# A third tile for every third gemv weight, laid in the attention's own pool

## The chip, the cores and the metric

The kernel runs on one core of a Trainium2 chip. What counts is the device time of one execution in microseconds; the figure before is the median of three runs.

## The reference, cut to what matters

A decoder trunk of two layers on 512 tokens of 1024 channels: layer 0 mixes tokens by stick-breaking attention, layer 1 by a diagonal state-space model, and each has a gated MLP with a short convolution behind it. Every sublayer is modulated by vectors computed from a conditioning vector `c`; that is the part that the change touches.

```
c_act = jax.nn.silu(c)
for i in range(DEPTH):
    mod = c_act @ w_mod[i] + b_mod[i]                      # (1024) @ (1024 x 6144)
    sh1, sc1, g1, sh2, sc2, g2 = jnp.split(mod, 6, axis=-1)
    h = modulate(rms_norm(x, norm_mix[i]), sh1, sc1)
    y = stick_breaking_attention(h, ...) if i == 0 else s5_ssm(h, ...)
    x = x + g1[:, None, :] * y
    h = modulate(rms_norm(x, norm_ffn[i]), sh2, sc2)
    x = x + g2[:, None, :] * conv_ffn(h, ...)
fin = c_act @ w_fin + b_fin
```

All arithmetic is float32; a product is made of three matmuls of split operands (high x high, low x high, high x low).

## The kernel before, in words

**The gemv.** `mod` and `fin` have 8192 outputs, which the kernel computes on DVE (VectorE), not on PE (TensorE): the transposed weights are cut into tiles of 128 outputs by 1024 inputs (512 KB), and for each tile one DVE instruction (L197, 1.2 us) multiplies it by `cact`, which holds silu(c) in every partition, and sums along the row into one column of `raw`. `gemv_step(col)` loads the tile and records that instruction; the tile is called `wg` and the column number (wg16 is the first one that the change concerns). The two tiles named `wg` that `gvp` (pool "gemv", right side of SBUF) holds are used in turn, so a load waits until the gemv two before it has been computed. When eight columns are done, `gemv_fin` (L204) adds the bias. The 16 columns that the first norm needs have a buffer of their own (`wgs`) and are not concerned.

**Where the gemvs stand in attention.** `bg(n)` takes the next n columns of a list and puts their gemvs at this place of the program. In attention the loads of wg16 to wg40 are issued by POOL (GpSimd, `queue=G`); all other large loads stand in the queue of SP (SyncE), each behind the one before it. POOL has nothing else to do there: its row of loads is a queue in which each waits for DVE to free a tile. The 16 heads are done in eight pairs. After the first (`window(0, ...)`, with three gemvs), pairs 1 to 6 are done by `middle(pr, ...)`, which writes the order out by hand: PE computes k and q of the next pair in 16 units of three matmuls, and between them the transposes (`t`), the products with v (`o`) of the pair before and the four rows of scores (`z`) of this pair. `follow` chains DVE's and ACT's instructions in the order in which they are written. On DVE that order is in each pair:

- two gemvs, the split of the next k weight (L165), a third gemv, the scans (`om`, L797) of rows 0 and 1, a fourth gemv,
- the low part of k (`kz`, L773), the split of the next q weight, the scans of row 2, the low part of q (`q_sq`, `q_nt`, L773), the scans of row 3.

The scans take what ACT (ScalarE) has put through a sigmoid out of the score's bank; `kz`, `q_sq` and `q_nt` read the bank of k or q, and free it. In the last of these pairs (`middle(6, ...)`) the two splits are those of the output projection's weights wo0, wo1 and wo2, and the low parts of the head outputs (`oL`, L927) stand between. Its gemvs are wg37, wg38, wg39 and wg40; those of the pair before are wg33 to wg36. PE then runs the first units of the output projection (`wo`, L170, L173, L174), which need `oL`, the split weights and free banks. `window(8, ...)` ends attention's pool; wg41 to wg44 stand ahead of it, loaded by SP.

**The start.** x comes in eight loads of 256 KB on SP. Each lets ACT square it and DVE add it up; after the last one PE sums over channels (`stat`), the reciprocal root is computed and spread (`dg`, `rbc`), and the value projection begins (L651). Dummy matmuls (`spare`, L1455) stand between. POOL issues wg16 and wg17 in these first microseconds, since their tiles have no reader before.

The order on each engine within a stretch is set by a scheduler where the code doesn't pin it; pools opened inside a stage give their space back at its end, and a later tile waits for the last reader of the bytes that it takes.

Of the kernel before, what the change touches and what calls it, by code (L numbers as in the profile page):

```python
# [2 lines left out]

# [4 lines left out]
F32 = mybir.dt.float32  # L8
# [8 lines left out]
P = 128  # L17
T = 512
D = 1024
# [69 lines left out]
def _trunk(ctx, tc, I, out, tap):  # L89
# [24 lines left out]
    gvp = gctx.enter_context(tc.tile_pool(name="gemv", bufs=1, side="right"))  # L114
# [21 lines left out]
    pin = {"head": []}  # L136
# [3 lines left out]
    def follow(eng, fn):  # L140
        with tc.issue_after(line[eng].ins) if eng in line else ExitStack():
            line[eng] = fn()
        return line[eng]


    def load_w(src, n=D, name="w", own=None, lined=False):
        raw = wp.tile([P, D], F32, tag="wraw", bufs=3, name=name + "_r")
        if isinstance(own, list):

            pin["load"] = SP.dma_start(raw, src)  # L150
            cols = slice(0, D // 2), slice(D // 2, D)
            for q, cs in enumerate(cols):
                pe_pin(S.activation(own[q], raw[:, cs], AF.Copy))
            for q, cs in enumerate(cols):
                pe_pin(V.tensor_tensor(own[2 + q], raw[:, cs], own[q].bitcast(F32), ALU.subtract))
            return own[:2], own[2:]
        if own:
            wh, wl = (own.tile([P, D], F32R, tag=name + g, name=name + g) for g in ("_h", "_l"))
        else:
            wh = wp.tile([P, D], F32R, tag="wH", bufs=NW, name=name + "_h")  # L160
            wl = wp.tile([P, D], F32R, tag="wL", bufs=NW, name=name + "_l")
        pin["load"] = SP.dma_start(raw[:, :n], src)
        order = follow if lined else lambda eng, fn: fn()
        order("S", lambda: S.activation(wh[:, :n], raw[:, :n], AF.Copy))  # L164
        pin["split"] = order("V", lambda: V.tensor_tensor(wl[:, :n], raw[:, :n], wh[:, :n].bitcast(F32), ALU.subtract))  # L165
        return wh, wl
# [24 lines left out]

    def gemv_step(col, pinned=True, w=None, load=True, lined=False, queue=SP):
        if w is None:
            w = gvp.tile([P, D], F32, tag="wg", bufs=2, name=f"wg{col}")
        if load:
            queue.dma_start(w, I["w_modT"][col * P:(col + 1) * P, :])
        mul = lambda: V.scalar_tensor_tensor(w, w, 1.0, cact, ALU.mult, ALU.mult, accum_out=raw[:, col:col + 1])  # L197
        ins = follow("V", mul) if lined else mul()
        if pinned and not lined:
            tc.keep_in_program_order(ins)  # L200

    def gemv_fin(col, n=KD):
        b = sm("b_mod", col, n) if col < 96 else sm("b_fin", col - 96, n)
        V.tensor_tensor(mod[:, col:col + n], raw[:, col:col + n], b, ALU.add)  # L204
# [10 lines left out]
    def bg(n, pinned=True, lined=False, queue=SP):  # L215
        while n > 0 and bgq:
            c, f = bgq.pop(0)
            if c is None:
                gemv_fin(f)
            else:  # L220
                gemv_step(c, pinned, lined=lined, queue=queue)
                n -= 1
        if bgq and bgq[0][0] is None:
            gemv_fin(bgq.pop(0)[1])
# [24 lines left out]
    def pe_pin(ins):  # L249
        tc.keep_in_program_order(ins)  # L250
# [90 lines left out]
    @contextmanager  # L341
    def behind_head(pins=None):
        with ExitStack() as st:
            for ins in pin["head"][-1] if pins is None else pins:
                st.enter_context(tc.issue_after(ins.ins))
            yield
# [194 lines left out]
    def attention(acc):  # L541
        with ExitStack() as av_, ExitStack() as ac:
# [22 lines left out]
            def high(k):  # L565
                w = [wp.tile([P, D], F32R, tag=f"w{g.upper()}", bufs=NW, name=f"wv{k}_{g}") for g in "hl"]
                pe_pin(S.activation(w[0], raws[k], AF.Copy))
                return w

            def gv_mul(v, k):  # L570
                gemv_step(mcol(0, v, k), True, wgs[:, (2 * k + 1 - v) % 4, :], False)
# [109 lines left out]
            w = high(1)  # L681
            for k in range(1, KD):
# [12 lines left out]
                w = nxt[0]  # L695
# [13 lines left out]
            warm = np_.tile([P, 64], F32, tag="warm", bufs=1, name="warm")[:, 0:1]  # L709
            pe_pin(S.activation(warm, ones[:, 0:1], AF.Sigmoid))  # L710
            ap = ac.enter_context(tc.tile_pool(name="attn", bufs=1, reuse_waits="tile"))

            kz = [[ap.tile([P, T], F32R, tag=f"kz{b}{h2}", name=f"kz{b}{h2}") for h2 in range(2)] for b in range(2)]
            for b in range(2):
# [143 lines left out]
            def wsrc(mt):  # L858
                return I["w_oa"][mt * P:(mt + 1) * P, :]
# [92 lines left out]
            window(7, wo_units(range(KPRE), range(3)), FILL7)  # L952
            with behind_head([pin["scan"]]):
                bg(4, False)

            early = {mt: load_w(wsrc(mt), name=f"wo{mt}", lined=True) for mt in (3, 4)}

# [507 lines left out]
    for k in range(KD):  # L1465
# [4 lines left out]
        if k:  # L1470
            pe_pin(V.tensor_tensor(acc, acc, sq, ALU.add))
    R = attention(acc)
    for k in range(KD):
        tap(f"x1_{k}", x[k])
# [161 lines left out]
```

## Time and profile before

| | |
|---|---|
| median of three runs | 1178.74 us (1178.59 to 1181.57) |
| profiled execution | 1178.0 us, of which the span of the trace is 1176.1 |
| mean granted clock of PE | 0.995 |
| busy in the span | PE 1156.7 us, DVE 858.0, ACT 564.1, POOL 272.5 |
| gemvs of the tiles `wg` (L197) | 96, 122.0 us busy, 28.7 us idle ahead of them for their loads |
| their loads | 71 by SP, 25 by POOL, 512 KB each |

A row of the trace gives the start in us from the span's start, the duration, the engine, the line of the code, the operation with output and inputs, and in brackets the engine's idle time just before it with what ended it. Times in the text are on the clock of this one profiled execution unless a median is named.

### The profile page before, as it was taken

The page shows a single profiled execution, that of the slowest core. Times are in us where ns is not written, and L with a number is a line of the kernel's source. Part 1 is how long each engine was busy: PE and PEld are TensorE (multiplying, and loading weights), DVE is VectorE, ACT ScalarE, POOL GpSimd, SP SyncE. Part 2 cuts the span into 40 slices and gives each one's busy share as a digit, 9 for nine tenths or more (in the row PEclk, how much of TensorE's full clock was granted, in tenths as well). Part 3 has the DMA queues.
Part 4 walks back from the last instruction along what each step waited for, and adds up shares of the span by engine and source line. Part 5 has one row for each costly group of instructions (what it writes and reads, how often), then busy time and mean ns, then how long its engine had stood idle before and what let it go on. Part 6 is the DMA issues. An engine that isn't in the chain of part 4 may idle for free.

```text
span 1176.1 us, 16597 instructions
## 1 busy us (share of the span) xinstructions
PE 1156.7 (98%) x6242; PEld 964.3 (82%) x6242; DVE 858.0 (73%) x1311; ACT 564.1 (48%) x896; POOL 272.5 (23%) x278
## 2 busy tenths in 40 slices
PE   8999998999999999999999999999999999999997
PEld 6888786799788878888889888789888888888887
DVE  6977989665998657697857599787598368744555
ACT  6756667456452234323445577647443144422443
POOL 2001110000298699979800000000000000000003
PEclk9999999999999999999999999999999999999999
DMA  9874554331267847788646598671166356432322
GB/s 342 289 244 136 187 177 164 104 130 55 73 188 266 254 148 235 217 279 277 226 145 211 169 339 308 204 253 54 53 224 220 110 152 180 136 124 72 92 69 72
DMA packets 91618, 211.01 MB, mean 179 GB/s; under 512 B 19601, under 2 KB 37905, under 8 KB 91538
## 3 DMA queue, kind: packets, MB, share of 16 engines
q1 hardware_dynamic: 78562, 191.08, 50.4%
q0 software_dynamic: 4656, 16.78, 4.5%
q10 hardware_dynamic: 8320, 2.10, 0.8%
q8 instruction: 49, 0.80, 0.3%
q14 instruction: 31, 0.25, 0.1%
HBM read 188.68 MB, written 21.24 MB: 178 GB/s over the span
## 4 chain that ended last, share of the span: by engine, by line
PE 67%; POOL 9%; issue 8%; DVE 7%; DMA 6%; ACT 2%; SPq 0%; POOLq 0%; DVEq 0%; ACTq 0%
PE up L170 11%; PE up L173 11%; PE up L174 11%; PE dn L170 5%; PE dn L173 5%; PE dn L174 5%; DMA wg<-in_w_modT_dram 2%; PE wo L170 1%; PE wo L173 1%; PE u L173 1%; PE wo L174 1%; PE u L170 1%; PE u L174 1%; PE wos L173 1%; PE wos L174 1%
## 5 line engine op out<-in xcount | busy, mean ns | idle before, releaser
L174 PE MATMUL up<-hH,up_l 128*128 128x512 f32 x640 | 249.4, 390 | 0.7 <-DVE up_l L165 0.7
L170 PE MATMUL up<-hH,up_h 128*128 128x512 f32 x640 | 249.7, 391 | 0.3 <-DVE ca L460 0.3
L173 PE MATMUL up<-hL,up_h 128*128 128x512 f32 x640 | 249.3, 390 | 0.0
L460 DVE SCALAR_TENSOR_TENSOR ca<-up,small,ca 128x511 f32<-128x511 f32 (+1 forms) x176 | 131.6, 748 | 120.5 <-ACT ca L458 117.2
L170 PE MATMUL dn<-gH,dn_h 128*128 128x512 f32 (+1 forms) x394 | 145.0, 369 | 0.0
L173 PE MATMUL dn<-gL,dn_h 128*128 128x512 f32 (+1 forms) x394 | 144.5, 367 | 0.0
L174 PE MATMUL dn<-gH,dn_l 128*128 128x512 f32 (+1 forms) x394 | 144.4, 366 | 0.0
L197 DVE SCALAR_TENSOR_TENSOR wg<-wg,cact 128x1024 f32<-128x1024 f32 x96 | 122.0, 1288 | 28.8 <-DMA wg<-in_w_modT_dram 28.7
L174 PEld LDWEIGHTS up<-hH,up_l 128*128 128x128 f32 x640 | 120.1, 188 | 26.4 <-DVE up_l L165 1.6
L170 PEld LDWEIGHTS up<-hH,up_h 128*128 128x128 f32 x640 | 120.1, 188 | 26.3 <-issue 1.7
L173 PEld LDWEIGHTS up<-hL,up_h 128*128 128x128 f32 x640 | 120.2, 188 | 24.4
L458 ACT ACTIVATE ca<-up,small 128x512 f32<-128x512 f32 x88 | 68.2, 775 | 148.0 <-PE up L174 148.0
L1508 POOL TENSOR_SCALAR xa<-x,Anorm_out 128x256 f32<-128x256 f32 x7 | 5.7, 817 | 569.9 <-DVE x L354 569.9
L164 ACT ACTIVATE up_h<-up_r 128x1024 fp32r<-128x1024 f32 x80 | 84.2, 1052 | 80.4 <-PE dn L173 57.3
L165 DVE TENSOR_TENSOR up_l<-up_r,up_h 128x1024 fp32r<-128x1024 f32 x80 | 113.4, 1417 | 10.3 <-ACT up_h L164 9.3
L354 DVE SCALAR_TENSOR_TENSOR x<-dn,mod,x 128x512 f32<-128x512 f32 (+1 forms) x55 | 37.4, 680 | 68.6 <-PE dn L174 68.6
L170 PEld LDWEIGHTS dn<-gH,dn_h 128*128 128x128 f32 x394 | 74.3, 188 | 12.7 <-issue 0.6
L174 PEld LDWEIGHTS dn<-gH,dn_l 128*128 128x128 f32 x394 | 74.3, 189 | 12.2
L173 PEld LDWEIGHTS dn<-gL,dn_h 128*128 128x128 f32 x394 | 74.3, 189 | 12.1
L164 ACT ACTIVATE dn_h<-dn_r 128x1024 fp32r<-128x1024 f32 (+1 forms) x48 | 46.7, 982 | 47.8 <-PE dn L173 38.0
L165 DVE TENSOR_TENSOR dn_l<-dn_r,dn_h 128x1024 fp32r<-128x1024 f32 (+1 forms) x48 | 63.3, 1318 | 2.2 <-ACT dn_h L164 2.0
L476 ACT ACTIVATE gH<-gm 128x512 fp32r<-128x512 f32 x44 | 27.1, 616 | 68.2 <-DVE gm L472 68.2
(349 smaller groups left out, 2311.4 us busy)
## 6 DMA issues: line engine op xcount, KB each, us to landing
up_r<-in_w_up_dram SPq DMA_DIRECT2D x80, 512.0 KB
wg<-in_w_modT_dram SPq DMA_DIRECT2D x71, 512.0 KB
dn_r<-in_w_down_dram SPq DMA_DIRECT2D x32, 512.0 KB
wg<-in_w_modT_dram POOLq DMA_DIRECT2D x25, 512.0 KB, 4.0
wgs<-in_w_modT_dram SPq DMA_DIRECT2D x16, 512.0 KB
dn_r<-in_w_down_dram SPq DMA_DIRECT2D x16, 384.0 KB
wv_r<-in_w_v_dram SPq DMA_DIRECT2D x8, 512.0 KB
wk_r<-in_w_qk_dram SPq DMA_DIRECT2D x8, 512.0 KB
```

The source lines that it names most:

```text
L164: order("S", lambda: S.activation(wh[:, :n], raw[:, :n], AF.Copy))
L165: pin["split"] = order("V", lambda: V.tensor_tensor(wl[:, :n], raw[:, :n], wh[:, :n].bitcast(F32), ALU.subtract))
L170: ins = PE.matmul(ps, ah, bh, start=start, stop=False)
L173: PE.matmul(ps, ah, bl, start=False, stop=False)
L174: PE.matmul(ps, al, bh, start=False, stop=stop)
L197: mul = lambda: V.scalar_tensor_tensor(w, w, 1.0, cact, ALU.mult, ALU.mult, accum_out=raw[:, col:col + 1])
L354: add = lambda: V.scalar_tensor_tensor(xs, pv, gate, xs, ALU.mult, ALU.add)
L458: follow("S", lambda: S.activation(ca, ps, AF.Identity, bias=small[:, cb:cb + 1], scale=tapw[2]))
L460: follow("V", lambda: V.scalar_tensor_tensor(ca[:, q:], ps[:, :T - q], tapw[2 - q], ca[:, q:], ALU.mult, ALU.add))
L476: follow("S", lambda: S.activation(gh, m, AF.Copy))
L1508: G.tensor_scalar(xa[k], x[k][:, cb], a[:, k:k + 1], 0.0, ALU.mult, ALU.add)
```

## The change

While attention's pool `ap` is open, `gemv_step` counts its calls, and the third, sixth and so on take a tile `wg3` of `ap` in place of one of the two of `gvp`. In that stretch a load so waits for the gemv three before it. `wg3` is another 4 KB per partition in `ap`. The stretch runs from wg16 to wg44; wg18, wg21 and so on to wg42 lie in the third tile.

```
-            w = gvp.tile([P, D], F32, tag="wg", bufs=2, name=f"wg{col}")
+            third = pin.get("third")
+            if third and next(third[1]) % 3 == 2:
+                w = third[0].tile([P, D], F32, tag="wg3", bufs=1, name=f"wg{col}")
+            else:
+                w = gvp.tile([P, D], F32, tag="wg", bufs=2, name=f"wg{col}")
...
             ap = ac.enter_context(tc.tile_pool(name="attn", bufs=1, reuse_waits="tile"))
+            pin["third"] = ap, count()
...
             window(7, wo_units(range(KPRE), range(3)), FILL7)
             with behind_head([pin["scan"]]):
                 bg(4, False)
+            pin["third"] = None
```

PE's instructions keep their order. On POOL, the row of loads at the start, before (`kz` and `maskb` are the attention's key tiles and mask, which are set here; `dg` belongs to the first norm):

```order
L716 MEMSET kz11_618 64x512
L196 DMA wg16_856<-in_w_modT_dram 128x1024
L196 DMA wg17_859<-in_w_modT_dram 128x1024
L698 ISA
L698 TENSOR_SCALAR maskb_108<-consts_87 128x128
L612 TENSOR_SCALAR dg_186<-consts_87,ny_208 128x128 x2
L196 DMA wg18_862<-in_w_modT_dram 128x1024
L196 DMA wg19_906<-in_w_modT_dram 128x1024
```

and now:

```order
L722 MEMSET kz11_618 64x512
L201 DMA wg16_856<-in_w_modT_dram 128x1024
L201 DMA wg17_859<-in_w_modT_dram 128x1024
L201 DMA wg18_862<-in_w_modT_dram 128x1024
L703 ISA
L703 TENSOR_SCALAR maskb_108<-consts_87 128x128
L617 TENSOR_SCALAR dg_186<-consts_87,ny_208 128x128 x2
L201 DMA wg19_906<-in_w_modT_dram 128x1024
```

The third load has moved ahead of the mask and of the first norm's `dg`, to the two that stood there. On SP, at the end of attention, the loads of the projection weights wo4 to wo7, of the last gemv weights and of the first MLP weight (`upo0`), before:

```order
L162 DMA wo4_r_2177<-in_w_oa_dram 128x1024
L150 DMA wo5_r_2226<-in_w_oa_dram 128x1024
L150 DMA wo6_r_2254<-in_w_oa_dram 128x1024
L162 DMA wo7_r_2355<-in_w_oa_dram 128x1024
L196 DMA wg43_2165<-in_w_modT_dram 128x1024
L196 DMA wg44_2168<-in_w_modT_dram 128x1024
L196 DMA wg45_3009<-in_w_modT_dram 128x1024
L162 DMA upo0_r_2365<-in_w_up_dram 128x1024
L196 DMA wg46_3140<-in_w_modT_dram 128x1024
```

and now:

```order
L201 DMA wg43_2165<-in_w_modT_dram 128x1024
L163 DMA wo4_r_2177<-in_w_oa_dram 128x1024
L151 DMA wo5_r_2226<-in_w_oa_dram 128x1024
L151 DMA wo6_r_2254<-in_w_oa_dram 128x1024
L163 DMA wo7_r_2355<-in_w_oa_dram 128x1024
L201 DMA wg44_2168<-in_w_modT_dram 128x1024
L201 DMA wg45_3009<-in_w_modT_dram 128x1024
L201 DMA wg46_3140<-in_w_modT_dram 128x1024
L163 DMA upo0_r_2365<-in_w_up_dram 128x1024
```

wg43 has moved ahead of four projection weights, and wg46 ahead of `upo0`. On DVE a few neighbours have changed places (wg43's gemv ahead of a split of wo5, small instructions of the MLP's preparation).

More of the change, by code (lines that the diff above doesn't have):

```diff
@@ L2 @@
 from contextlib import ExitStack, contextmanager
+from itertools import count
 import concourse.bass as bass
```

## The prediction

> **What bounds the kernel now.** I read the page's busy table first, then the waits of each engine, then the granted clock by stretches, and then the order in time on DVE, ACT, POOL and PE around the one place that stood out.
>
> ```profile
> span 1176.1 us, 16597 instructions
> PE 1156.7 (98%) x6242; PEld 964.3 (82%) x6242; DVE 858.0 (73%) x1311; ACT 564.1 (48%) x896; POOL 272.5 (23%) x278
> ...
> POOL wg L196 <- DVE wg L197: 150.0, 21, 74.7
> ...
> DVE wg L197 <- DMA wg<-in_w_modT_dram: 17.4, 12, 3.1
> ```
>
> The last two rows are the waits between 85 and 235 us (total us, times, longest). DVE stands 17.4 us in front of gemv weights that have not landed, and POOL, which issues those loads, stands for DVE to free a tile. That looks like a gain of 17 us. It is not, because PE is busy for 98% of the span, and a DVE wait counts only where PE waits behind it. The next table (stretch: length, busy us of PE, PEld, DVE, ACT and POOL, then the granted clock, DMA share and GB/s) shows where that is.
>
> ```profile
> 20.40:198.40 178.00, 178.00 (x906) 143.06 (x904) 150.89 (x220) 118.60 (x219) 12.20 (x23) 1.00 0.62 209
> 198.40:208.70 10.30, 6.67 (x18) 4.83 (x18) 10.24 (x14) 4.67 (x8) 0.00 (x0) 0.67 0.30 104
> ...
> 235.00:262.00 27.00, 27.00 (x186) 25.07 (x183) 18.00 (x34) 12.69 (x20) 0.00 (x0) 1.00 0.44 145
> ...
> 200.00:202.00 2.00, 1.26 (x5) 0.69 (x5) 2.00 (x3) 1.82 (x4) 0.00 (x0) 0.91 0.92 371
> 202.00:204.00 2.00, 0.38 (x1) 0.41 (x2) 1.94 (x4) 1.24 (x2) 0.00 (x0) 0.50 0.17 70
> 204.00:206.00 2.00, 2.00 (x6) 1.52 (x6) 2.00 (x3) 0.00 (x0) 0.00 (x0) 0.50 0.03 8
> ```
>
> From 20.4 to 198.4 PE has no idle time at all, so DVE's waits there are free. From 198.4 to 208.7 PE idles while DVE is full, and the clock falls to half: a mean of 0.91 from 200 to 202 puts the fall at about 201.6. From 235 PE is full again. PE in order of time there (start, duration, instruction, idle before it and its releaser):
>
> ```profile
> 198.17 0.39 PE L170 MATMUL wo<-oH,wo_h 128*128 128x512 f32 x1
> 199.82 0.50 PE L173 MATMUL wo<-oL,wo_h 128*128 128x512 f32 x1 [1.26 <-DVE oL L927]
> ...
> 200.40 0.39 PE L170 MATMUL wo<-oH,wo_h 128*128 128x512 f32 x1
> 200.63 0.40 PE L173 MATMUL wo<-oL,wo_h 128*128 128x512 f32 x1
> ...
> 203.62 0.77 PE L170 MATMUL wo<-oH,wo_h 128*128 128x512 f32 x1 [2.36 <-DVE q_nt L773]
> ...
> 204.61 0.63 PE L174 MATMUL wo<-oH,wo_l 128*128 128x512 f32 x1
> 205.04 0.63 PE L170 MATMUL wo<-oH,wo_h 128*128 128x512 f32 x1
> ...
> 208.70 1.93 PE L809 MATMUL t<-consts,om 128*128 128x128 f32 x14
> ```
>
> These are the first six units (18 matmuls) of the output projection. Start to start a matmul takes 0.23 us at full clock (200.40 to 200.63) and 0.43 at half (204.61 to 205.04). The 18 take 198.17 to 208.70, 10.53 us; at full clock without a stall they take 18 x 0.23 = 4.14. So this place holds **6.4 us**: 4.0 in two stalls, both released by DVE, and 2.4 in the half clock that follows. It is all that this change can reach.
>
> **The change: why DVE is late there.** DVE and POOL ahead of it:
>
> ```profile
> 171.71 1.23 DVE L197 SCALAR_TENSOR_TENSOR wg<-wg,cact 128x1024 f32<-128x1024 f32 x1 [2.06 <-DMA wg<-in_w_modT_dram]
> ...
> 175.91 1.23 DVE L197 SCALAR_TENSOR_TENSOR wg<-wg,cact 128x1024 f32<-128x1024 f32 x1 [1.15 <-DMA wg<-in_w_modT_dram]
> ...
> 183.00 2.34 DVE L797 TENSOR_TENSOR_SCAN om<-om,maskb 128x512 f32<-128x512 f32 x2
> 185.25 1.20 DVE L197 SCALAR_TENSOR_TENSOR wg<-wg,cact 128x1024 f32<-128x1024 f32 x1
> ...
> 190.84 1.22 DVE L197 SCALAR_TENSOR_TENSOR wg<-wg,cact 128x1024 f32<-128x1024 f32 x1 [2.10 <-DMA wg<-in_w_modT_dram]
> ...
> 192.19 0.73 DVE L797 TENSOR_TENSOR_SCAN om<-om,maskb 128x128 f32<-128x128 f32 x2
> ...
> 195.39 0.68 DVE L773 TENSOR_TENSOR kz<-k,kA 64x512 fp32r<-64x512 f32 x1
> ...
> 202.78 0.69 DVE L773 TENSOR_TENSOR q_nt<-q,q_nt 64x512 fp32r<-64x512 f32 x1
> ```
>
> ```profile
> 186.76 0.53 POOL L196 DMA_DIRECT2D wg<-in_w_modT_dram  x1 [8.79 <-DVE wg L197]
> 187.90 0.53 POOL L196 DMA_DIRECT2D wg<-in_w_modT_dram  x1 [0.62 <-DVE wg L197]
> ...
> DMA to landing us min/median/max: 3.7/4.0/7.0
> ```
>
> Weight wg39 (used at 190.84) may load only once wg37 (185.25) has been used, at 186.76, and lands 4.0 us later. With three tiles in rotation it waits for wg36 (175.91) instead and lies there in time: **the 2.10 us wait goes**. wg40 then waits for wg37; by the worst landing, 7.0 after 186.76, it arrives at 193.8, and 2.85 us sooner when DVE runs as far ahead as below. So the wait doesn't move to wg40.
>
> The waits of the pair of heads before (2.06 and 1.15) go in the same way, as do those of earlier pairs. How far ahead does DVE get? Until its next input, which ACT writes from PE's banks on PE's clock:
>
> ```profile
> 179.58 1.09 ACT L796 ACTIVATE om<-z 128x512 f32<-128x512 f32 x2
> ...
> 187.35 1.13 ACT L796 ACTIVATE om<-z 128x128 f32<-128x128 f32 x4
> ...
> 190.17 0.59 ACT L771 ACTIVATE kB<-k 64x512 fp32r<-64x512 f32 x1
> ```
>
> The scan at 183.00 can start when the first of the two ACT rows at 179.58 is done, about 180.15: 2.85 us earlier, less than the 3.21 of the two waits. The pair of gemvs then starts at 182.40. The scan of row 0 stood at 192.19; less 2.10 and 2.85 that is 187.24, but ACT gives its row at about 187.7, so 0.45 is lost: kz starts at 195.39 - 4.5 = 190.9, after ACT's 190.76. From kz to the end of q_nt DVE runs without a gap, 203.47 - 195.39 = 8.08, so q_nt ends at 199.0. PE comes to the unit that needs it at 198.17 + 6 x 0.23 = 199.55. Both stalls go, the second with only 0.5 us to spare, and without a stall nothing halves the clock: **-6.4 us**. The other end: if DVE enters the last pair no earlier and gains its own 2.10 alone, q_nt ends at 201.4, PE saves 4.4 with the full clock and 2.1 with half. I take the upper end because the early start is bounded by rows that stand in the trace.
>
> What is late next: the transposes (208.70, now 202.3) need the last scan of that pair, which follows q_nt by 2.34 and so ends at 201.4. Behind it PE is full again from 235, with nothing there tied to an absolute time, so the gain is kept.
>
> **What it adds: a third load in the first microseconds.** The third weight no longer waits, so POOL issues it behind the two at the start instead of at 93.5 us. The start is bound by transfers. The fence has POOL's two loads, the chain's step, ACT at the last x tile, PE at that tile, and the two DMA queues in 9 to 10 and in 11 to 12 us (packets, MB, share of the 16 engines).
>
> ```profile
> 3.52 1.29 POOL L196 DMA_DIRECT2D wg<-in_w_modT_dram  x2
> ...
> 4.42 7.75 DMA x<-in_xT_dram
> ...
> 12.26 0.63 ACT L1467 ACTIVATE sq<-x 128x512 f32<-128x512 f32 x1 [1.01 <-DMA x<-in_xT_dram]
> ...
> 12.22 0.71 PE L1455 MATMUL spare<-x,ones 128*128 128x128 f32 x4 [0.93 <-DMA x<-in_xT_dram]
> ...
> q0 software_dynamic: 78, 0.29, 72.2%
> q1 hardware_dynamic: 74, 0.12, 31.8%
> ...
> q1 hardware_dynamic: 119, 0.42, 102.3%
> q0 software_dynamic: 6, 0.01, 2.2%
> ```
>
> While POOL's two loads run (q0), x gets 0.12 MB/us; once they end, near 11 us, it gets 0.42, and the last x lands at 12.2. A third load of 0.52 MB at 0.29 MB/us keeps q0 going for 1.8 us more. Whichever way the queues share, the engines are full at about 0.41 MB/us, so x and all behind it come up to 0.52 / 0.41 = **+1.3 us** later. x is on the chain, and PE has no gap from 20.4 to 198.4, so this is paid in full. The other end is 0 (if the third load trails x). I take 1.3, by the shares in 9 to 10 us. The Trainium skill, "DMA: Bandwidth & Descriptors", section on queues, rings and completion order, says that a DMA engine takes its queues in turn, packet by packet; by that rule x waits too, and the 1.3 stands; the shares above agree.
>
> The rest is free: the adds and multiplies are the same, PE's order is unchanged, the tile is 4 KB of a partition, and the load of wg43 that now stands in front of a projection weight on SP waits for wg40's gemv, which DVE does before the split that frees that weight's buffer.
>
> **Sum.** -6.4 + 1.3 = -5.1 us. The profiled execution took 1178.0 (span 1176.1 and 1.9 around it), 0.7 under the median of 1178.74. From the median: **1173.6 us**, -0.43%.
>
> **Rivals.**
> 1. *DVE gains only its own wait* in the last pair (an input that I overlooked holds it). Then -4.4 or -2.1, with +1.3: 1175.6 or 1177.9. For it: the spare time of 0.5 us is thin. Against: ACT's rows above. 15%.
> 2. *The clock halves at the start, and it ends slower.* Around 200 us the clock fell at 201.6, after idle stretches of 1.4 and 0.5 us with 1.3 of work between. At the start PE would wait 0.93 + 1.3 = 2.2 us for the last x: emptier. If the half clock lasted only through the dummy matmuls, it costs 0 to 2, giving 1173.6 to 1175.6 (13%). Each matmul of the value projection behind it costs 0.20 more. From 25 of these on (one block of 24 takes 5.4 us) the gain is gone; with two whole blocks, 48 x 0.20 = 9.6, it ends at 1183.2 (7%). Against: at 203.62 a steady run got the clock back within 4.9 us, and the dummies come before. The Trainium skill, "TensorE: Matmul & The Clock Gate", section on HAM oscillation, sets its rule of thumb at idle gaps over 3.4 us; by it the 2.2 us at the start would be harmless and the sum stay -5.1. But by it the clock would not have halved at 201.6 either, where no gap passes 2.5, so the row decides and the rival stays.
> 3. *The third load is hidden*: x has landed before its packets begin. 1172.3. Against: q0's shares above. 10%.
> 4. *The wait returns later*, at wg44 or the first FFN weights behind it on SP. Some 2 to 4 us given back: 1175.6 to 1177.6. 5%.
>
> **Chances.** The forecast (1173.6, give or take 1.2) has 50%. 0.3% is 3.5 us here, about what a measurement can tell from no change. Faster by more: most of the forecast's 50, all of rival 3 and a few of 2 and 4, 60%. Slower: the far end of 2 and what I don't see, 8%. Within: 32%. The range goes from rival 3 and a little more gain, 1171.5, to rival 1's bad end, 1178.6.
>
> **What would show it.** Right: no DVE wait for wg between 104 and 195; no PE wait on q_nt and oL; clock 1.00 from 198 to 212; the transposes, 10.5 us behind the first wo matmul now, 4 us behind it; last x at about 13.5 and the first value matmul at 21.5. Wrong: x as before; a clock of 0.50 before 30 us; PE still waiting for q_nt; a new wait on L196 of SP after 218.

## The result, and the profile after

| | before | after |
|---|---|---|
| median of six runs, same chip | 1180.55 us (1178.59 to 1181.57) | 1172.50 us (1171.55 to 1178.13) |
| after / before | | 0.9943, 95% interval 0.9922 to 0.9963 |
| profiled execution, and its span | 1178.0, 1176.1 | 1172.41, 1170.6 |

The ratio is worked out from the single runs; it is not the quotient of the two medians, which is 0.9932. Of the executions counted below two were slow, at a granted clock of 0.848 and 0.671 (1277.03 us, of the kernel with the extra load only, and 1604.98 us, of before); medians and counts hold them, ratios do not.

The forecast was 1173.6. The profiled execution became 5.6 us shorter, and its span 5.5; the forecast sum was 5.1.

All times below are on the clock of the profiled execution named. First the page's head, the changed kernel:

```profile
span 1170.6 us, 16595 instructions
PE 1156.1 (99%) x6242; PEld 966.5 (83%) x6242; DVE 855.1 (73%) x1311; ACT 564.7 (48%) x896; POOL 274.0 (23%) x278
```

PE's busy time is as before (1156.7); what went is PE's idle time. The waits between 85 and 235 us (total us, times, longest):

```profile
POOL wg L201 <- DVE wg L202: 150.8, 20, 74.9
...
DVE om L803 <- ACT om L802: 8.8, 10, 2.4
...
DVE wg L202 <- DMA wg<-in_w_modT_dram: 3.2, 2, 2.0
```

DVE's waits for weights fell from 17.4 us in twelve to 3.2 us in two. In their place stand longer waits for ACT (5.0 us in three before, 8.8 in ten now): the scans wait for the rows that ACT writes, as the forecast had it. POOL waits as long as before, 150 us of it, which says nothing. The stretches (length, then busy us of PE, PEld, DVE, ACT and POOL, granted clock, DMA share, GB/s):

```profile
11.50:14.91 3.41, 2.41 (x12) 2.12 (x11) 1.39 (x2) 0.97 (x2) 0.00 (x0) 0.50 1.04 410
...
15.00:20.00 5.00, 5.00 (x25) 5.00 (x25) 2.87 (x8) 1.60 (x5) 1.17 (x2) 0.50 1.03 410
...
22.50:200.30 177.80, 177.80 (x908) 143.42 (x907) 155.34 (x225) 118.80 (x220) 11.67 (x22) 1.00 0.63 214
200.34:204.44 4.10, 4.10 (x20) 3.33 (x19) 4.05 (x6) 4.10 (x7) 0.00 (x0) 1.00 0.00 0
```

The last row is the place of the forecast. PE in order of time there: the first unit of the output projection, the third (which needs q's bank, that is, the end of `q_nt`), and the transposes behind the 18 matmuls.

```profile
200.34 0.39 PE L171 MATMUL wo<-oH,wo_h 128*128 128x512 f32 x1
...
201.71 0.39 PE L171 MATMUL wo<-oH,wo_h 128*128 128x512 f32 x1
...
204.44 0.82 PE L815 MATMUL t<-consts,om 128*128 128x128 f32 x6
```

No row carries a wait. The 18 matmuls take 4.10 us in place of 10.53, and the clock stays full. DVE ahead of them:

```profile
182.43 2.34 DVE L803 TENSOR_TENSOR_SCAN om<-om,maskb 128x512 f32<-128x512 f32 x2 [0.98 <-ACT om L802]
184.69 1.20 DVE L202 SCALAR_TENSOR_TENSOR wg<-wg,cact 128x1024 f32<-128x1024 f32 x1
...
188.10 1.22 DVE L202 SCALAR_TENSOR_TENSOR wg<-wg,cact 128x1024 f32<-128x1024 f32 x1
...
191.72 1.20 DVE L202 SCALAR_TENSOR_TENSOR wg<-wg,cact 128x1024 f32<-128x1024 f32 x1
192.97 0.68 DVE L779 TENSOR_TENSOR kz<-k,kA 64x512 fp32r<-64x512 f32 x1
...
200.37 0.69 DVE L779 TENSOR_TENSOR q_nt<-q,q_nt 64x512 fp32r<-64x512 f32 x1
```

The four gemvs of the last pair stand there without a wait for their weights (the third, at 188.10, is wg39's). The pair begins at 184.69, although PE is 2.2 us later than before. `q_nt` ends at 201.06 and PE needs it at 201.71: 0.65 us to spare.

The start went the other way. POOL's loads, ACT at the last x tile, PE from the last x tile to the first value matmul, and the two queues in 9 to 10 and in 11 to 12 us (packets, MB, share of the 16 engines):

```profile
3.52 1.82 POOL L201 DMA_DIRECT2D wg<-in_w_modT_dram  x3
```
```profile
13.16 0.63 ACT L1474 ACTIVATE sq<-x 128x512 f32<-128x512 f32 x1 [1.32 <-DMA x<-in_xT_dram]
```
```profile
11.17 0.95 PE L1462 MATMUL spare<-x,ones 128*128 128x128 f32 x4 [2.06 <-DMA x<-in_xT_dram]
...
20.11 1.83 PE L622 MATMUL rbc<-dg,ones 128*128 128x256 f32 x4
...
22.59 0.71 PE L656 MATMUL v<-wv_h,hH 128*128 128x512 f32 x2
```
```profile
q0 software_dynamic: 75, 0.26, 65.4%
q1 hardware_dynamic: 75, 0.14, 37.2%
...
q0 software_dynamic: 78, 0.27, 66.3%
q1 hardware_dynamic: 75, 0.16, 40.4%
```

In 11 to 12 us q0 still moves 0.27 MB, where before it was done (0.01), and x gets 0.16 MB/us in place of 0.42. The two queues move about as many packets there (78 and 75), but q0's are the larger, so x gets the smaller part of the bytes. The last x comes 0.9 us later. But the first value matmul comes 2.4 us later (20.17 before): the rest is the half clock of the two rows 11.50:14.91 and 15.00:20.00 above, which lasts to 21.74 here and which this execution of before did not have. At half clock the 16 dummies behind `stat` take 3.76 us in place of 2.03, and `rbc` comes right behind them.

Since PE's 6242 matmuls keep their order, the two traces can be laid side by side matmul by matmul. After less before: +0.9 us at the last x, +2.2 to +2.4 from the norm to the first projection matmul, -4.3 behind the 18 matmuls, -4.8 at 322 us, -5.6 at the last matmul.

### The profile page after: what moved, and what is told of

It reads as the page before. It is cut to its first block, busy times and chain, and to the rows that moved or that the text cites. A ratio compares the mean times of both kernels' runs of the same rounds, so it can differ in the third digit from the quotient of the medians.

```text
span 1170.6 us, 16595 instructions
## 1 busy us (share of the span) xinstructions
PE 1156.1 (99%) x6242; PEld 966.5 (83%) x6242; DVE 855.1 (73%) x1311; ACT 564.7 (48%) x896; POOL 274.0 (23%) x278
## 4 chain that ended last, share of the span: by engine, by line
PE 80%; POOL 8%; DMA 4%; DVE 4%; ACT 1%; issue 1%; SPq 0%; POOLq 0%; ACTq 0%; DVEq 0%
PE up L171 11%; PE up L174 11%; PE up L175 11%; PE dn L171 5%; PE dn L174 5%; PE dn L175 5%; PE o L831 2%; PE t L815 2%; PE wo L171 1%; PE u L174 1%; PE u L171 1%; PE wo L174 1%; PE wo L175 1%; PE u L175 1%; PE q L175 1%
## 5 line engine op out<-in xcount | busy, mean ns | idle before, releaser
L166 DVE TENSOR_TENSOR dn_l<-dn_r,dn_h 128x1024 fp32r<-128x1024 f32 (+1 forms) x48 | 60.5, 1261 | 1.6 <-ACT dn_h L165 1.3
```

## The experiments

After this trace three things were open. Is the loss at the start the late x alone, or does the third load also halve the clock there? Is the whole saving at the projection due to wg39's own wait, or is the early entry of DVE into the last pair needed too? And what is the change worth without its cost at the start? The table has the profiled execution of each kernel: ACT's last square of x, the spread norm (`rbc`), the first value matmul, the time from the first `wo` matmul to the transposes, the number of 3.41 us stretches at half clock (at the start, at the projection, near 430 us; that length is explained in the last section), and the span.

| kernel | last x | rbc | first v | wo to t | half clock | span | median (runs) | ratio to before |
|---|---|---|---|---|---|---|---|---|
| before | 12.26 | 17.83 | 20.17 | 10.53 | 0/2/0 | 1176.1 | 1180.55 (6) | |
| before_again | 12.44 | 19.13 | 21.39 | 9.14 | 2/1/0 | 1175.4 | 1177.24 (1) | |
| after | 13.16 | 20.11 | 22.59 | 4.10 | 3/0/0 | 1170.6 | 1172.50 (6) | 0.9943 |
| after_again | 14.57 | 21.52 | 23.79 | 4.10 | 3/0/0 | 1171.7 | 1173.05 (6) | 0.9948 (0.9931 to 0.9966) |
| third load later | 12.64 | 18.76 | 21.11 | 4.10 | 1/0/1 | 1173.5 | 1174.47 (7) | 0.9943 (0.9923 to 0.9964) |
| all three loads later | 10.01 | 14.92 | 17.26 | 4.10 | 0/0/0 | 1165.3 | 1167.22 (5) | 0.9887 (0.9868 to 0.9906) |
| extra load only | 13.47 | 20.27 | 22.46 | 9.85 | 2/1/1 | 1181.1 | 1182.32 (12) | 1.0011 (0.9997 to 1.0025) |
| third tile for wg39 alone | 12.25 | 19.09 | 21.13 | 5.48 | 2/0/0 | 1172.5 | 1176.31 (10) | 0.9964 (0.9951 to 0.9977) |
| more dummies | 14.34 | 20.68 | 23.02 | 4.10 | 1/0/0 | 1171.2 | 1170.87 (6) | 0.9922 (0.9906 to 0.9938) |
| two tiles, loads later | 10.3 | 16.64 | 18.45 | 10.57 | 1/2/1 | 1177.4 | 1177.18 (12) | 0.9985 (0.9967 to 1.0003) |

The first four experiments ran on one chip, where before had a median of 1180.22 us in 22 runs (1177.09 to 1183.76), the others on another, with 1179.96 in 17.

**Only the third tile's first load later.** wg18's load goes behind the first norm's `dg` on POOL, where before had it; all else is as in the changed kernel.

```
-            queue.dma_start(w, I["w_modT"][col * P:(col + 1) * P, :])
+            with tc.issue_after(pin["dgp"].ins) if queue is G and col == 18 else ExitStack():
+                queue.dma_start(w, I["w_modT"][col * P:(col + 1) * P, :])
...
-                        G.tensor_scalar(dst, ident, y[:, i:i + 1], 0.0, ALU.mult, ALU.add)
+                        pin["dgp"] = G.tensor_scalar(dst, ident, y[:, i:i + 1], 0.0, ALU.mult, ALU.add)
```

> The change, with the third tile's first load (wg18) put behind the first norm's dg on POOL; all else as in the change. Theory A (the change is the sum of two independent parts: -6.4 us at the first units of the output projection from the third tile, and +2.2 us at the start from the third load, 0.9 of it late x and 1.3 half clock): last x at about 12.2 us, clock 1.00 through the start, projection's first matmul at 198.2 as in the kernel before, its six units in 4.1 us; time 7.5 to 8.0 us under the kernel before. Theory B (late x and half clock at the start come and go between executions and have nothing to do with the third load): the start stays 2 us late in this kernel too, 5.5 us under the kernel before.

Measured: the last x comes at 12.64 and the first value matmul at 21.11, 1.5 us before the changed kernel's; the projection is the same 4.10. The start is given back later, most of it near 427 us, in the preparation of the second layer, where PE waits for POOL (waits of PE between 420 and 445; then the stretch before the clock halves):

```profile
PE pk L1145 <- POOL cl L1208: 1.7, 1, 1.7
```
```profile
424.51:427.92 3.41, 1.75 (x21) 0.87 (x20) 0.00 (x0) 0.21 (x1) 3.25 (x3) 1.00 1.00 354
```

The changed kernel waits 0.9 us at the same place and keeps its clock. Laid beside the changed kernel's trace, this one is 1.5 us ahead up to 427 us and 0.9 behind at 442; two gaps of PE near 666 and 717 us (0.76 and 1.11), which that trace doesn't have, and what follows them put it 2.9 behind at the end. The seven runs lie between 1169.58 and 1176.67, around the changed kernel's; the median (1174.47) shows no gain, and the 7.5 to 8.0 us under before that theory A expected did not come. The cost at the start is confirmed in the trace of the start, and not in the time. Whether the other runs lose the gain at the same places is open, since only one was profiled.

**All three first loads later.** The same edit with `col in (16, 17, 18)`.

> As the run before, with all three first loads (wg16, wg17, wg18) behind dg on POOL, so that none runs beside x. Theory A (the loads beside x cost what their bytes cost, 0.52 MB at 0.41 MB/us each): last x at 9.6 to 10.5 us, the value projection 1.7 to 2.6 us earlier than in the kernel before, time 9 to 10.4 us under it. Rival: the 1.6 MB meet the value weights at 20 to 40 us, where the transfers are 0.9 to 1.0 full; PE waits up to 1.6 / 0.41 = 3.8 us there, and the time is 4 to 8 us under the kernel before. Theory B: no different from the run before.

Measured: 1167.22, the best of all, 5 to 6 us under the changed kernel's two medians; its ratio's interval lies clear of both of theirs. The last x comes at 10.01 and the first value matmul at 17.26, 5.3 us before the changed kernel's, and the span is 5.3 shorter. The three loads now run beside the value projection, issued at 15.8 to 17.6, and land later than before, at no cost to PE (stretches, then the answer on the tile `wg` for 0 to 30 us):

```profile
7.67:11.09 3.42, 2.89 (x20) 2.28 (x19) 2.98 (x5) 2.25 (x4) 0.00 (x0) 1.00 1.03 380
...
17.20:195.10 177.90, 177.90 (x907) 143.30 (x907) 155.29 (x225) 118.35 (x220) 12.11 (x23) 1.00 0.65 226
```
```profile
DMA to landing us min/median/max: 8.7/10.5/12.5
```

The clock is full from 4.3 us to the last microseconds. The gain is more than either theory expected (13 us under before in the medians, 10.9 by the spans of the two profiles). Beside the profile of before, 2.9 us of it come at the start, 6.4 at the projection, 0.5 up to 322 us and 1.0 near 430. Two things follow: the third load beside x delays the start, and the two that before has as well together delay it more (the first value matmul moves from 22.59 to 21.11 and then to 17.26).

**The extra load alone.** Before with one more load of 512 KB behind the two at the start, into a tile that nobody reads.

```
-                bg(BGA, queue=G)
+                bg(2, queue=G)
+                G.dma_start(ap.tile([P, D], F32, tag="wg3", name="wgx"), I["w_modT"][18 * P:19 * P, :])
+                bg(BGA - 2, queue=G)
```

> The kernel before with one extra load of 512 KB behind wg17's on POOL at the start, into a tile that nobody reads; two tiles for the gemvs as before. Theory A: last x at 13.1 us, half clock for two or three stretches of 3.4 us from some 11 to 12 us on, the value projection and all behind it 1 to 2.3 us later: 1 to 2.3 us over the kernel before. Theory B: no difference from the kernel before.

Measured: 1182.32, ratio 1.0011 with an interval that holds 1. In the trace the last x comes 1.2 us later than before and the first value matmul 2.3 later, which is the changed kernel's delay.

```profile
13.47 0.63 ACT L1469 ACTIVATE sq<-x 128x512 f32<-128x512 f32 x1 [1.31 <-DMA x<-in_xT_dram]
```

So the delay is the load's and not the tile's. How much of it reaches the median is not settled: 1.3 us is the middle of the interval, -0.4 and +3.0 its ends.

**The third tile for wg39 alone.** Only the weight whose wait the forecast named gets the third tile, and its load stands behind wg38's; the start and all earlier pairs are as before.

```
-            if third and next(third[1]) % 3 == 2:
+            if third and col == 39:
...
-            queue.dma_start(w, I["w_modT"][col * P:(col + 1) * P, :])
+            with tc.issue_after(pin["gload"].ins) if col == 39 else ExitStack():
+                ld = queue.dma_start(w, I["w_modT"][col * P:(col + 1) * P, :])
+            if col == 38:
+                pin["gload"] = ld
```

> The change for one weight alone: only wg39 lies in the third tile, with its load behind wg38's on POOL; every other gemv weight in the two tiles. DVE enters the last pair as late as before and is spared its 2.10 us wait there. Start as before. If what counts is both DVE's own wait and its early entry from the pairs ahead (theory A): q_nt ends at 201.4, PE waits about 1.9 us for it, 4.4 us under the kernel before with the full clock and 2.1 with half. If the own wait alone did it: 6.4 under. If the early entry alone did it: 0 to 1 under.

Measured: 1176.31, ratio 0.9964, which is 4.2 us. DVE's first gemv of the last pair, PE at the projection, and the stretch with its stall:

```profile
187.01 1.20 DVE L205 SCALAR_TENSOR_TENSOR wg<-wg,cact 128x1024 f32<-128x1024 f32 x1
...
203.25 0.47 PE L171 MATMUL wo<-oH,wo_h 128*128 128x512 f32 x1 [1.10 <-DVE q_nt L782]
...
206.10 1.92 PE L818 MATMUL t<-consts,om 128*128 128x128 f32 x14
```
```profile
200.10:203.51 3.41, 2.31 (x10) 1.61 (x10) 3.35 (x6) 3.36 (x7) 0.00 (x0) 1.00 0.60 227
```

Of the two stalls, the first is gone and the second has shrunk from 2.36 to 1.10 us. The clock stays full, with PE busy for 2.31 us of the 3.41. The 18 matmuls take 5.48 us, 5.0 less than in before. Not all of it is the wait's: PE waited 1.0 us for DVE's scans ahead of this place and came to it 13.6 us behind the pair's first gemv, where before has 12.9. Less these 0.7 us, the wait alone gives about 4.4, as expected. The other 2 us need the early entry of DVE, which the waits taken away from the pairs before give. Both parts of the forecast's mechanism are real, and one wait alone is most of it.

**More dummies.** The changed kernel, with eight more dummy matmuls behind each of the sixth and seventh x tiles, to keep the clock at the start.

```
-        idle(NIDLE[1], x[k])
+        idle(NIDLE[1] + (8 if k in (5, 6) else 0), x[k])
```

> The change with 16 more dummy matmuls on PE while the last two x tiles are awaited (8 behind the sixth tile, 8 behind the seventh). Theory A2 (the last x comes 0.9 to 1.2 us late for the third load's bytes; the half clock at the start is a thing of its own, it follows from PE being empty while it waits for x, and comes in some executions of every kernel): x still late at 13.1, clock 1.00 through the start, the first norm's rbc at 18.6 to 18.9 against 20.1 in the change's profile, time 1.0 to 1.5 us under the change's. Rival (the half clock comes from something else than PE's idle time): half clock from 11 to 22 us as in the change's profile, same time as the change.

Measured: 1170.87, ratio 0.9922; the middle is 2.2 us under the changed kernel's on the same chip (0.9948), the intervals overlap. In its profiled execution, the slowest of its six, the edit missed its aim (PE, and the stretch before the clock halves):

```profile
10.68 6.81 PE L1462 MATMUL spare<-x,ones 128*128 128x128 f32 x44 [1.21 <-DMA x<-in_xT_dram]
17.77 0.95 PE L270 MATMUL stat<-ones,acc 128*128 128x1 f32 x8
```
```profile
7.76:11.18 3.42, 1.21 (x8) 1.02 (x9) 1.45 (x3) 1.09 (x2) 0.00 (x0) 1.00 1.01 392
```

The emptiest stretch lies ahead of the new dummies, so the clock halves at 11.18 all the same, and the dummies, at half speed, hold `stat` back to 17.77. But it is back after one stretch in place of three. The mean clock of its six runs is 0.997 to 0.999, against 0.994 to 0.996 for the changed kernel beside it.

**Two tiles, loads later.** Before, without the third tile, with the loads of wg16 and wg17 behind `dg`.

> The kernel before, two tiles, with its two first loads (wg16, wg17) put behind dg on POOL. It is the start alone, without the third tile. Theory A2: last x at 10.0, clock 1.00 at the start, rbc at 14.9 as in the run with all three later; the projection's first matmul to the transposes still 10.5 us with both stalls and half clock; 2.9 us under the kernel before's profile, 3 to 5 under its median. If start and projection were not independent (an earlier start only makes DVE wait longer later), 0 to 1 under.

Measured: 1177.18, ratio 0.9985 with an interval that holds 1. The start is 1.7 us shorter (first value matmul at 18.45), the projection has both stalls (10.57), and the clock halves at the start and near 433 (stretches before each fall):

```profile
9.82:13.24 3.42, 2.63 (x21) 2.27 (x21) 3.13 (x4) 1.08 (x2) 1.11 (x1) 1.00 1.04 404
429.67:433.08 3.41, 1.25 (x19) 0.64 (x19) 0.00 (x0) 0.00 (x0) 3.25 (x3) 1.00 0.90 264
```

Its runs reach from 1171.30 to 1181.82. That lies between the two expectations. So taking the loads from the start is worth 0.6% with the third tile and, without it, 0.15%, which these runs can't tell from nothing. The trace of this one execution loses its gain again at 430; whether the others do is open.

**The changed kernel and before again**, for a second profile of each beside these.

> The change unaltered, for more executions on one chip beside the others and a second profile. Theory A2: 5 to 7 us under the kernel before; last x at 13.0 to 13.5 again; one to three stretches of 3.4 us of half clock at the start; none at the projection.

> The kernel before unaltered, for a second profile. Theory A2: last x at 12.2 again; 10.5 us from the projection's first matmul to the transposes again, with half clock there; at the start perhaps one or two stretches of half clock, since a kernel with the same first 90 us on every engine showed two. If the third load alone makes the half clock at the start: none.

Measured: 1173.05 for the changed kernel, and the same picture: 4.10 at the projection, three stretches of half clock from 12.30. Of before, the second profile differs from the first at the start (the stretch before the clock falls, of before_again, of after_again, and of the first profile of before, where it didn't fall):

```profile
9.81:13.23 3.42, 1.54 (x11) 1.35 (x12) 1.53 (x4) 1.26 (x2) 0.00 (x0) 1.00 1.04 406
```
```profile
8.89:12.31 3.42, 0.76 (x5) 0.52 (x4) 1.36 (x2) 0.63 (x1) 0.00 (x0) 1.00 1.04 416
```
```profile
10.50:13.92 3.42, 2.13 (x15) 1.75 (x15) 1.73 (x3) 1.26 (x2) 0.00 (x0) 1.00 1.04 402
```

Before has the half clock at the start too, without any third load; the profile on which the forecast rested was an execution that happened to escape it. Against before_again the changed kernel's first value matmul is 1.2 us later in its first profile and 2.4 in its second.

## Why the prediction was right, and where its terms were off

**The two stalls and the half clock behind them (-6.4).** Right to the number against the profile it was made on: 10.53 to 4.10 is 6.43. It held in all five profiles with the third tile throughout (4.10 each). The steps hold too: no wait of DVE for a weight between 104 us and the end of the projection, the scan in front of the pair waiting for ACT (0.98), the pair 2.7 us earlier against PE than before (forecast 2.85), the third unit met with 0.65 us to spare (forecast 0.5). What one profile hid is that the term varies: with two tiles the place took 10.53, 9.14, 9.85 and 10.57 in four executions, by one or two stretches of half clock, so it is worth 5.0 to 6.5 from one execution to the next.

**The bound from below (-4.4).** DVE gaining its own wait alone gave about 4.4 in the experiment with wg39, once the 0.7 us by which PE was late there are taken off; the bound was right (by the forecast's own figures, 6.4 less a wait of 1.8, it is 4.6). The changed kernel got 6.43, so the choice of the upper end was right, and rival 1 is out.

**The third load (+1.3).** Right in its mechanism and in its size for x: two loads at the start put the last x at 12.25 to 12.64 (four profiles), three at 13.16 to 14.57 (four), none at 10.01 and 10.3. By the means, 12.4, 13.9 and 10.2, each load costs 1.1 to 1.5 us, though two profiles of the changed kernel alone lie 1.4 apart. In the runs the term isn't shown: the extra load's interval holds 1, and moving the third load behind `dg` left the ratio at 0.9943.

What was mis-sized is the way from x to the norm. The forecast carried x's delay through unchanged; in this pair of profiles the first value matmul was 2.4 us late, since between the last x and `rbc` there lie 5.6 us at full clock (before) and 6.7 to 7.0 with two or three stretches of half clock (before_again, the wg39 kernel, after, after_again). That is the mild branch of rival 2, which had 13%. With it came one of the forecast's signs of being wrong, a clock of 0.50 before 30 us, and the first value matmul stands at 22.59 in place of 21.5. But its cause was only partly as told there. The half clock does not need the third load, since two kernels with before's start show it as well. That the third load prolongs it isn't shown: the changed kernel has three stretches and these two have two, but the extra load alone has two as well, and the stretch before the fall isn't always emptier with it (1.36 and 0.76 us busy in the changed kernel, 1.54 and 1.07 in those two). Rival 2's severe branch, half clock in the value projection, did not occur: it is full from 22.5. Rival 3, a hidden load, is out by the row of q0.

**The wait that returns later (rival 4).** It does not: at the four gemvs of wg41 to wg44 DVE waits 1.24 us (226.11), where before waited 1.10 and 0.67 (230.03 and 232.53), and no wait of PE hangs on it (0.3 us of PE's waits between 195 and 262 in all). What speaks against it in the forecast's account, that PE is full from 235, held.

**Nothing tied to absolute time behind it.** Right: behind the projection the lead grows from 4.3 to 5.6 us, by 0.6 to 322 us and by 0.7 after it, in small pieces that the forecast did not have and that no run took apart.

**The sum.** In the profile, -6.4 + 2.2 - 0.6 - 0.7 = -5.5, against -5.1: the start 0.9 worse, the rest 1.3 better. That the sum came so near is in part luck: the two errors offset each other, and no run explains the second. In the runs the gain is 0.57% and 0.52%, 6.7 and 6.1 us, above the profile's and the forecast's. Why is open. That the usual execution of before has the half clock at the start, and its first profile hadn't, doesn't explain it: before_again has it, and its span is still 0.7 us shorter. Both profiled executions of before (1178.0 and 1177.24) were faster than its medians; the runs without a profile show only a mean clock.

## What to carry to other kernels

A wait of 17 us on an engine was worth 6.4, and the place to read that from was the one stretch where TensorE waited behind it; there a third buffer for a single tile gives most of it. A buffer that is free at the start makes its load start at the start: hold back the loads that are needed late (all three were first used near 94 us) until the input has landed, which here was worth another 5 to 6 us in the medians. And one profile is one draw: where a term rests on the granted clock, take a second profile before you size it.

## What the runs showed of the hardware

**The clock is decided stretch by stretch of 3.41 us, and the phase of the stretches changes with the execution.** Ahead of the idle end, half clock came in lengths of one, two or three times 3.41 us in nine of the ten profiles, and not at all in the tenth (all three loads later). Laid from the moment at which the clock first became full (4.67 us in after, 7.09 in before), the falls stand on that grid: before's at 201.65 is 57 stretches behind 7.09. The stretch that ends at the fall decides. In the ten profiles 14 stretches at full clock, counted to 1154 us, had PE busy for 1.75 us or less of the 3.41, and the clock fell behind each of the 14; of the 26 with 2.07 to 2.74 us it fell behind one (9.82:13.24 of two tiles, loads later, 2.63 us busy), and why it did is open. Of before, the fall at the projection:

```profile
198.24:201.66 3.42, 1.75 (x7) 0.86 (x5) 3.42 (x5) 3.25 (x6) 0.00 (x0) 1.00 0.69 236
```

So about the same idle time halves the clock in one execution and not in another: over the two stretches around the last x tiles PE was busy for 4.9 us in before, shared as 2.76 and 2.13, and for 4.8 in before_again, shared as 3.25 and 1.54. The kernel is the same, so the half clock at the start can come and go without the change. It fits the spread of the runs: 3.0 to 10.5 us in the kernels that show half clock, 1.8 us in the one that shows none (five runs). How long the clock stays down isn't told by the busy time: it was back after one stretch of 3.41 us busy (11.18 of more dummies) and after two (12.37 of the third tile for wg39 alone).

The Trainium skill, "TensorE: Matmul & The Clock Gate", section "What's actually happening", gives a free-running window of 3413 ns, whose place differs from run to run; the trace agrees, with 3.41 us and the phases above. The Trainium skill, on the same page, section "HAM oscillation — how this bites in real kernels", makes an idle gap of over 3.4 us the danger; here the trace differs: behind single waits of at most 2.06 us (after, at 11.17) and of 1.26 (before, at 199.82) the clock fell. In these runs the busy time of a stretch told a fall better than its longest gap: the wait of 1.26 us in before went with a fall, and one of 1.63 in more dummies (at 428.95, 1.35 of it in a stretch busy for 2.07) went without.

**A load whose packets share the engines with x delays x by about its bytes at the full rate**, 1.1 to 1.5 us for 512 KB by the profiles (0.52 MB at 0.41 MB/us is 1.3): three loads held back by 12 us gave the start 5.3 us, the half clock that went with them included, and landing in 8.7 to 12.5 us cost nothing behind the norm.
